# Layer-1 mixer of a two-layer decoder: the preparation split into a part of k and a part of q and v, and the chain begun once k is there

## The chip, the cores and the metric

The kernel runs on one core of a Trainium2 chip. The metric is device microseconds of one execution, median of several. TensorE (PE in the profile) does the matmuls and transposes, VectorE (DVE) and ScalarE (ACT) work on what comes out, GpSimd (POOL) does a few small powers, and the DMA issues stand on SyncE (SP).

## The reference

The program computes a decoder trunk of two layers on 256 tokens of width 1024. The change concerns the mixer of layer 1, a chunked gated DeltaNet with 8 heads of 128, in chunks of 64 tokens. Cut to what matters:

```python
def mixer_c(x, w_in, conv_w, a_log, dt_bias, norm_g, w_out):
    h = x @ w_in
    q, k, v, z, bl, al = _split(h, P1_SPLITS)
    qkv = jax.nn.silu(causal_dwconv(jnp.concatenate([q, k, v], axis=-1), conv_w))
    q, k, v = _split(qkv, P1_SPLITS[:3])
    o = gated_deltanet(q, k, v, bl, al, z, a_log, dt_bias, norm_g)
    return o @ w_out

# in gated_deltanet, per head and chunk
gc = jnp.cumsum(scal(g), axis=-1)
decay = exp(where(incl, gc[..., :, None] - gc[..., None, :], -inf))
m = jnp.where(strict, einsum('bhntk,bhnsk->bhnts', kb, kh) * decay, 0.0)
tinv = triangular_solve(eye + m, eye)
u = tinv @ (vh * beta);  w = tinv @ (kb * exp(gc))
qk = einsum('bhntk,bhnsk->bhnts', qh, kh) * decay
# then a scan over the chunks: v_new = u - w state; out = qg state + qk v_new; state update
```

The triangular inverse needs k, beta and g alone. q and v come in with `u`, `qk` and the scan.

## The kernel before, in words

Every product is made in a split form: a weight tile is cast to a short part `wh` on ACT (L151), the rest `wl` is a subtraction on DVE (L153), and three matmuls are added (L158 to L160, L164 to L166). A tile of a projection of q, k or v is 128 output columns: 24 matmuls of 256 columns on PE, one cast on ACT, one subtraction on DVE, then a scale on ACT (L926), three taps of a short convolution on DVE (L929) and a silu on ACT (L934). There are four buffers each for `wh` and `wl`, so the cast for a tile waits until PE is done with the tile four before it.

The eight heads go in two groups of four. For each group `gdn_pre` prepares (twice, for two halves of 128 tokens): `pg` is the running sum of the decay, spread out by matmuls; `pk`, `pq`, `pv` are k, q, v turned by PE transposes; `dT` is the decay (DVE L1014, then an Exp on ACT, L1016); sums of squares of k and q (`sq`, ACT L999); `LT` is the matrix k k^T times beta and decay (DVE L1052), turned into `pL`. `gdn_inv` then doubles the block of the triangular inverse in six levels, each with two half-steps on PE: `pA` and `pX`, then `pZ`; between them ACT and DVE make the operands. `gdn_rec` runs the scan over the chunks (`pvn`, `pS`, `pon`) and the norm.

`scalars` makes beta and the decays. It is a chain across the engines: a small projection, `pl` on PE (L899), Abs, Exp and Ln on ACT (L905 to L907), `gg` on DVE (L913), `pgc` on PE (L917), then two results of `pgc` on ACT (`ngc`, `egs`, L919 and L920). The four silu of the first k projection (`ck`) are held back until `egs` is out.

What sets the order: before the first `yield 0` of `mixer_c` a scheduler places the instructions of all engines. From there on `weave` fixes the order on PE as it is written: at each `yield n` of the chain, n pieces of the fill (6 matmuls of a q, k or v projection, or 3 of a z projection, each) are put on PE. `steps` runs two or three generators of the chain in turn and adds their numbers; where a generator yields nothing, the weight from the list `NW` counts. The other engines' queues are still placed by the scheduler. Each engine works through its queue in order.

Before the change, k, q and v of group 0 are projected ahead of the chain, k, q and v of group 1 are fill for the preparation and inverse of group 0, and the z projection of group 1 is fill for the preparation and inverse of group 1, in which the scan of group 0 also runs.

Of the kernel before, what the change touches and what calls it, by code (L numbers as in the profile page):

```python
# [17 lines left out]
P = 128  # L18
# [11 lines left out]
NTAIL = 8  # L30
NEARLY = 6
AHEAD = 2
NW = [3, 2.6, 1, 2.5, 1, 1.2, 0.7, 3, 2, 3, 4, 1, 6, 2, 0, 5.2, 0.3, 3]
NEG = -1e30

def _constants():
# [52 lines left out]
def hybrid_trunk(ctx: ExitStack, tc: tile.TileContext, a: dict, const: dict, out: bass.AP, dbg=None):  # L89
# [778 lines left out]
    def mixer_c(h, hT, sm, smq, fill, res):  # L868
# [127 lines left out]
        def sum_sq(dst, src):  # L996
            junk = t2("sq")
            for g in range(4):
                nc.scalar.activation(junk[:, g], src[:, g], AF.Square, accum_out=dst[:, g:g + 1])  # L999

        def gdn_pre(grp, tt, o):
            tsl = slice(tt * P, tt * P + P)
            cs = slice(tt * 8 + grp * 4, tt * 8 + grp * 4 + 4)
            q, k, v = (qkvT[x, grp][:, :, tsl] for x in "qkv")
            sc = sm.tile([P, 6, 4], F32, tag="sc", name="sc", bufs=4)

            pg = bank("pg")
            mm4(pg, lambda g: gg[:, tt, grp * 4 + g:grp * 4 + g + 1].broadcast_to([P, P]), lambda g: tri)
            pk = bank("pk")
            tr4(pk, k)  # L1010
            dT = o["att"] = keep("dT", grp, tt)
            for g in range(4):
                i = tt * 8 + grp * 4 + g
                nc.vector.scalar_tensor_tensor(dT[:, g], pg[:, g], ngc[:, i:i + 1], dmask, op0=ALU.add, op1=ALU.min)  # L1014
            with tc.issue_after(table[1].ins):
                nc.scalar.activation(dT, dT, AF.Exp)  # L1016
                if tt:
                    qg = o["qg"] = keep("kq", grp, tt)
                    nc.scalar.activation(qg, pg, AF.Exp)
            sum_sq(sc[:, 0], pk)  # L1020
            if tt:
                kgx = o["kgx"] = g2("kgx")
                tts(kgx, pk, col(egs[:, 0, cs]), op=ALU.mult)
            else:
                kg = o["kg"] = keep("kq", grp, tt)
                tts(kg, pk, col(egs[:, 1, cs]), op=ALU.mult)
            yield NW[7 + grp]
            pq = bank("pq")
            tr4(pq, q)
            sum_sq(sc[:, 1], pq)  # L1030
            pv = bank("pv")
            tr4(pv, v)

            nc.vector.tensor_scalar(sc[:, 0:2], sc[:, 0:2], RMS_EPS, None, op0=ALU.add)
            nc.gpsimd.tensor_tensor(sc[:, 2], sc[:, 0], phalf, op=ALU.pow)
            nc.vector.reciprocal(sc[:, 3], sc[:, 0])
            nc.vector.tensor_tensor(sc[:, 3], sc[:, 3], beta[:, tt, grp * 4:grp * 4 + 4], op=ALU.mult)
            nc.vector.tensor_scalar(sc[:, 4], sc[:, 1], RMS_EPS * P, None, op0=ALU.mult)  # L1040
            o["b"], o["eq"] = sc[:, 3], sc[:, 4]
            vx = o["vx"] = keep("vx", grp, tt)
            for g in range(4):
                nc.scalar.mul(vx[:, g], pv[:, g], sc[:, 2, g:g + 1])
            if tt:
                tts(qg, qg, q, op=ALU.mult)
            yield
            pK = bank("pK")
            mm4(pK, lambda g: k[:, g], lambda g: k[:, g])
            LT = t2("LT")  # L1050
            for g in range(4):
                nc.vector.scalar_tensor_tensor(LT[:, g], pK[:, g], sc[:, 3, g:g + 1], dT[:, g],  # L1052
                                               op0=ALU.mult, op1=ALU.mult)
            pQ = bank("pQ")
            mm4(pQ, lambda g: k[:, g], lambda g: q[:, g])
            tts(dT, pQ, dT, op=ALU.mult)
            yield

            pL = bank("pL")
            tr4(pL, LT)  # L1060
            L = o["L"] = t2("L")
            nc.scalar.copy(L, pL)

            Z = o["Z"] = t2("Z")
            nc.scalar.copy(Z, row(C("ident1")))
            A = level_tile()
            zu = Z.rearrange("p g (u r b) -> p g u r b", u=2, r=2)[:, :, :, 1]
            tts(A, LT.rearrange("p g (n u) -> p g n u", u=2)[..., 1], heads(C("imask")), op=ALU.mult)
            tts(zu, zu, A.rearrange("p g (b u) -> p g u b", u=2), op=ALU.subtract)
            yield  # L1070

        def gdn_inv(o):
            Z, L = o["Z"], o["L"]
            for lev in range(1, NLEV + 1):

                last = lev == NLEV
                half = slice(0, 64)
                rows = slice(64, P) if last else slice(0, P)
                cols = half if last else slice(0, P)
                Lc = smq.tile([P, 4, 64], F32, tag="Lc", name="Lc", bufs=3)  # L1080
                nc.scalar.copy(Lc.rearrange("p g (r b) -> p g r b", r=1 << lev)[rows],
                               lower(L, lev)[rows].rearrange("p g b r -> p g r b"))
                pA = mm("pA")[half, :256].rearrange("p (g t) -> p g t", g=4)
                mm4(pA, lambda g: Lc[rows, g], lambda g: Z[rows, g, 64:])
                A = level_tile()[half]
                if last:
                    nc.vector.tensor_copy(A, pA)
                else:
                    tts(A, pA, heads(cmasks[half, lev - 1]), op=ALU.mult)
                pX = bank("pX")[half, :, cols]  # L1090
                for g in range(4):
                    nc.tensor.transpose(pX[:, g], Z[cols, g, half], ident[cols, cols])
                X = t2("X")[half, :, cols]
                nc.scalar.copy(X, pX)
                if not last:
                    def packed(x):
                        return x.rearrange("p g (i u) -> p g u i", u=2)

                    Z2 = g2("Z") if lev == NLEV - 1 else t2("Z")
                    Zv = Z2.rearrange("p g (u v i) -> p g u v i", u=2, v=2)  # L1100
                    nc.scalar.copy(Zv[:, :, :, 0], packed(Z[:, :, half]))
                yield
                pZ = mm("pZ")[cols, :256].rearrange("p (g t) -> p g t", g=4)
                mm4(pZ, lambda g: X[:, g], lambda g: A[:, g])
                if last:
                    tts(Z[half, :, 64:], Z[half, :, 64:], pZ, op=ALU.subtract)
                else:
                    tts(Zv[:, :, :, 1], packed(Z[:, :, 64:]), packed(pZ), op=ALU.subtract)
                    Z = o["Z"] = Z2
                yield NW[9] if "kgx" in o and lev == NLEV else None  # L1110
            if "kgx" in o:
                pw = bank("pw")
                mm4(pw, lambda g: o["kgx"][:, g], lambda g: Z[:, g])
                wT = o["wT"] = g2("wT")
                nc.scalar.mul(wT, pw, -1.0)
# [66 lines left out]
        run(extra)  # L1182
        for finish in late:
            finish()
        proj_t(*proj_c(0, "q"))
        proj_t(*proj_c(0, "v"))

        def group_1():
            for nm in "kqv":
                yield from proj_t_gen(*proj_c(1, nm))  # L1190

        yield 0
        fill.gens.append(group_1())
        yield from steps(NW[3], gdn_pre(0, 0, os_[0][0]), gdn_pre(0, 1, os_[0][1]))
        yield from steps(NW[4], gdn_inv(os_[0][0]), gdn_inv(os_[0][1]))
        fill.rest()
        fill.gens.append(proj_z(1))
        yield from steps(NW[5], gdn_pre(1, 0, os_[1][0]), gdn_pre(1, 1, os_[1][1]))
        outs = []
        yield from steps(NW[16], gdn_inv(os_[1][0]), gdn_inv(os_[1][1]), gdn_rec(0, os_[0], outs))  # L1200
        fill.rest()
        new = new_t("oT")
        oT.hi, oT.lo = new.hi, new.lo
# [246 lines left out]
```

## Time and profile before

| | |
|---|---|
| runs | 943.89 us median of 3 (941.56 to 945.12) |
| profiled execution | 942.03 us, of which the span of instructions is 940.3 us |
| PE busy | 917.3 us (98%), 6284 matmuls |
| weight loads on PE | 820.6 us (87%) |
| DVE busy | 689.1 us (73%) |
| ACT busy | 532.6 us (57%) |
| DMA | 152.89 MB, mean 163 GB/s |

PE is the engine to follow: its queue is in order and it is hardly ever idle. A matmul's end is modelled, so one row's time is longer than the distance to the next start; the pace is read from the distance of starts. The layer-1 mixer lies between about 480 us and 688 us of the span: k, q and v of group 0 from 490.6 us to 525.7 us, the preparation of group 0 up to 551.1 us, its inverse up to 596.1 us, the preparation of group 1 up to 615.5 us, its inverse together with the scan of group 0 up to about 654 us, then the scan of group 1 between the matmuls of the output projection.

### The profile page before, as it was taken

The page shows a single profiled execution, that of the slowest core. Times are in us where ns is not written, and L with a number is a line of the kernel's source. Part 1 is how long each engine was busy: PE and PEld are TensorE (multiplying, and loading weights), DVE is VectorE, ACT ScalarE, POOL GpSimd, SP SyncE. Part 2 cuts the span into 40 slices and gives each one's busy share as a digit, 9 for nine tenths or more (in the row PEclk, how much of TensorE's full clock was granted, in tenths as well). Part 3 has the DMA queues.
Part 4 walks back from the last instruction along what each step waited for, and adds up shares of the span by engine and source line. Part 5 has one row for each costly group of instructions (what it writes and reads, how often), then busy time and mean ns, then how long its engine had stood idle before and what let it go on. Part 6 is the DMA issues. An engine that isn't in the chain of part 4 may idle for free. (4 is left out here: it accounts for less than half of the span.)

```text
span 940.3 us, 15842 instructions
## 1 busy us (share of the span) xinstructions
PE 917.3 (98%) x6284; PEld 820.6 (87%) x6284; DVE 689.1 (73%) x1155; ACT 532.6 (57%) x945; POOL 36.0 (4%) x49
## 2 busy tenths in 40 slices
PE   6999999999999999999999999999999999999996
PEld 5887798889988999998889999888889789999885
DVE  5497586776458999984687975754697889999554
ACT  4753466445444766663357876664364476666440
POOL 1000001000000000000010100000200000000000
PEclk9999999999999999999999999997999999999998
DMA  7843345555573566655566441211444546665541
GB/s 247 293 147 108 117 135 183 177 180 179 190 251 97 180 198 209 209 193 182 179 189 190 136 127 54 91 46 45 151 163 136 177 137 213 207 206 182 189 170 45
DMA packets 101715, 152.89 MB, mean 163 GB/s; under 512 B 5225, under 2 KB 73673, under 8 KB 101641
## 3 DMA queue, kind: packets, MB, share of 16 engines
q1 hardware_dynamic: 99576, 145.08, 46.9%
q0 software_dynamic: 2064, 6.80, 2.2%
q8 instruction: 50, 0.82, 0.4%
q14 instruction: 25, 0.20, 0.1%
HBM read 150.81 MB, written 1.05 MB: 162 GB/s over the span
## 5 line engine op out<-in xcount | busy, mean ns | idle before, releaser
L153 DVE TENSOR_TENSOR wl<-raw,wh 128x1024 fp32r<-128x1024 f32 x268 | 325.4, 1222 | 116.0 <-ACT wh L151 113.3
L151 ACT CAST wh<-raw 128x1024 fp32r<-128x1024 f32 x268 | 278.9, 1052 | 229.3 <-PE ps_f L159 53.1
L158 PE MATMUL ps_f<-hT,wh 128*128 128x256 f32 x576 | 159.0, 276 | 0.0
L159 PE MATMUL ps_f<-hT,wh 128*128 128x256 f32 x576 | 159.0, 276 | 0.0
L160 PE MATMUL ps_f<-hT,wl 128*128 128x256 f32 x576 | 159.0, 276 | 0.0
L158 PEld LDWEIGHTS ps_f<-hT,wh 128*128 128x128 f32 x576 | 108.1, 188 | 0.0
L159 PEld LDWEIGHTS ps_f<-hT,wh 128*128 128x128 f32 x576 | 108.1, 188 | 0.0
L160 PEld LDWEIGHTS ps_f<-hT,wl 128*128 128x128 f32 x576 | 108.1, 188 | 0.0
L158 PE MATMUL ps_t<-hT,wh 128*128 128x256 f32 x352 | 100.5, 286 | 0.0
L159 PE MATMUL ps_t<-hT,wh 128*128 128x256 f32 x352 | 97.9, 278 | 0.0
L160 PE MATMUL ps_t<-hT,wl 128*128 128x256 f32 x352 | 97.8, 278 | 0.0
L164 PE MATMUL ps_o<-wh,aT 128*128 128x512 f32 x176 | 69.2, 393 | 0.0
L165 PE MATMUL ps_o<-wl,aT 128*128 128x512 f32 x176 | 68.8, 391 | 0.0
L166 PE MATMUL ps_o<-wh,aT 128*128 128x512 f32 x176 | 68.6, 390 | 0.0
L158 PEld LDWEIGHTS ps_t<-hT,wh 128*128 128x128 f32 x352 | 66.1, 188 | 0.7
L159 PEld LDWEIGHTS ps_t<-hT,wh 128*128 128x128 f32 x352 | 66.4, 189 | 0.1
L160 PEld LDWEIGHTS ps_t<-hT,wl 128*128 128x128 f32 x352 | 66.3, 188 | 0.0
L302 PE MATMUL ps<-wh,hT 128*128 128x512 f32 x192 | 54.3, 401 | 0.0
L302 PEld LDWEIGHTS ps<-wh,hT 128*128 128x128 f32 x192 | 36.0, 191 | 8.4 <-DVE hT L381 0.5
L1311 ACT ACTIVATE fy<-ps_f,fcw 128x256 f32<-128x256 f32 x72 | 40.2, 559 | 0.0
L164 PEld LDWEIGHTS ps_o<-wh,aT 128*128 128x128 f32 x176 | 33.0, 188 | 7.6 <-issue 0.5
L166 PEld LDWEIGHTS ps_o<-wh,aT 128*128 128x128 f32 x176 | 33.0, 188 | 7.3
(359 smaller groups left out, 1843.0 us busy)
## 6 DMA issues: line engine op xcount, KB each, us to landing
raw<-in_ffn_w_in SPq DMA_DIRECT2D x44, 1024.0 KB, 5.5
raw<-in_w_in SPq DMA_DIRECT2D x26, 1024.0 KB, 5.7
raw<-in_ffn_w_out SPq DMA_DIRECT2D x22, 1024.0 KB, 5.0
raw<-in_xa_wkv SPq DMA_DIRECT2D x16, 1024.0 KB, 5.3
raw<-in_w_mix_out SPq DMA_DIRECT2D x8, 1024.0 KB, 5.1
raw<-in_xa_wq SPq DMA_DIRECT2D x8, 1024.0 KB, 7.9
raw<-in_xa_wo SPq DMA_DIRECT2D x8, 1024.0 KB, 5.0
lngb<-in_ln_g POOLq DMA_DIRECT2D x6, 512.0 KB, 4.5
```

The lines of the kernel that those rows point to most:

```text
L151: nc.scalar.copy(hi, src)
L153: nc.vector.tensor_tensor(lo, src, hi.bitcast(F32), op=ALU.subtract)
L158: nc.tensor.matmul(ps, lh, rh, start=first, stop=False)
L159: nc.tensor.matmul(ps, lh, rl, start=False, stop=False)
L160: nc.tensor.matmul(ps, ll, rh, start=False, stop=last)
L164: nc.tensor.matmul(ps, lh, rh, start=first, stop=False)
L165: nc.tensor.matmul(ps, lh, rl, start=False, stop=False)
L166: nc.tensor.matmul(ps, ll, rh, start=False, stop=last)
L302: nc.tensor.matmul(ps, x, ww[:, k], start=k0 + k == 0 and ww is wh and not xl, stop=k0 + k == KT - 1 and ww is wl)
L1311: nc.scalar.activation(yt, ps, AF.Identity, scale=cw[:, 2, mc:mc + 1], bias=cw[:, 3, mc:mc + 1])
```

## The change

`gdn_pre` becomes `gdn_pre_k`, with all that the inverse needs, and `gdn_pre_q`, with the rest (`pq`, `pv`, `pQ`). The chain starts after the k projection of group 0. One list of fill holds q and v of group 0, then k, q and v of group 1, then z of group 1; `until` gives fill until a named projection is complete. The order of the chain is k part of group 0, inverse of group 0, q part of group 0, k part of group 1, inverse of group 1 with the scan of group 0, q part of group 1. The weights in `NW` are new.

```diff
-NW = [3, 2.6, 1, 2.5, 1, 1.2, 0.7, 3, 2, 3, 4, 1, 6, 2, 0, 5.2, 0.3, 3]
+NW = [3, 2.6, 1, 1.5, 1, 1, 0.7, 1, 1, 8, 4, 1, 6, 2, 0, 5.2, 0.5, 3]
...
-        def gdn_pre(grp, tt, o):
+        def gdn_pre_k(grp, tt, o):
...
-            yield NW[7 + grp]
-            pq = bank("pq")
-            tr4(pq, q)
-            sum_sq(sc[:, 1], pq)
-            pv = bank("pv")
-            tr4(pv, v)
+            yield
-            nc.vector.tensor_scalar(sc[:, 0:2], sc[:, 0:2], RMS_EPS, None, op0=ALU.add)
+            nc.vector.tensor_scalar(sc[:, 0], sc[:, 0], RMS_EPS, None, op0=ALU.add)
...
-            pQ = bank("pQ")
-            mm4(pQ, lambda g: k[:, g], lambda g: q[:, g])
-            tts(dT, pQ, dT, op=ALU.mult)
             yield
...
+        def gdn_pre_q(grp, tt, o):
...
+            pq = bank("pq")
+            tr4(pq, q)
+            sum_sq(sc[:, 1], pq)
+            pv = bank("pv")
+            tr4(pv, v)
+            nc.vector.tensor_scalar(sc[:, 4], sc[:, 1], RMS_EPS, RMS_EPS * P, op0=ALU.add, op1=ALU.mult)
+            vx = o["vx"] = keep("vx", grp, tt)
+            for g in range(4):
+                nc.scalar.mul(vx[:, g], pv[:, g], sc[:, 2, g:g + 1])
+            if tt:
+                tts(o["qg"], o["qg"], q, op=ALU.mult)
+            yield
+            pQ = bank("pQ")
+            mm4(pQ, lambda g: k[:, g], lambda g: q[:, g])
+            tts(dT, pQ, dT, op=ALU.mult)
+            yield
...
-                yield NW[9] if "kgx" in o and lev == NLEV else None
+                yield
...
-        proj_t(*proj_c(0, "q"))
-        proj_t(*proj_c(0, "v"))
+        made = set()
+        def fills():
+            for grp in range(2):
+                for nm in "kqv"[1 - grp:]:
+                    yield from proj_t_gen(*proj_c(grp, nm))
+                    made.add((nm, grp))
+        def until(nm, grp):
+            while (nm, grp) not in made:
+                yield 1
...
         yield 0
-        fill.gens.append(group_1())
-        yield from steps(NW[3], gdn_pre(0, 0, os_[0][0]), gdn_pre(0, 1, os_[0][1]))
-        yield from steps(NW[4], gdn_inv(os_[0][0]), gdn_inv(os_[0][1]))
-        fill.rest()
-        fill.gens.append(proj_z(1))
-        yield from steps(NW[5], gdn_pre(1, 0, os_[1][0]), gdn_pre(1, 1, os_[1][1]))
+        fill.gens += [fills(), proj_z(1)]
+        yield from units(NW[3], gdn_pre_k, 0)
+        yield from inv(NW[4], 0)
+        yield from until("v", 0)
+        yield from units(NW[7], gdn_pre_q, 0)
+        yield from until("k", 1)
+        yield from units(NW[5], gdn_pre_k, 1)
         outs = []
-        yield from steps(NW[16], gdn_inv(os_[1][0]), gdn_inv(os_[1][1]), gdn_rec(0, os_[0], outs))
+        yield from steps(NW[8], *(gdn_inv(os_[1][tt]) for tt in range(2)), gdn_rec(0, os_[0], outs))
+        yield from until("v", 1)
+        yield from units(NW[8], gdn_pre_q, 1)
         fill.rest()
```

**PE, the start of the chain.** Before, the scalars' `pl` is followed by the q projection of group 0 (`ps_t`), and 49 of its matmuls stand between `pl` and `pgc`; another 143 stand between `pgc` and `pg`.

```order
L899 MATMUL pl<-c_all,linT 128x16 x4
L158 MATMUL ps_t<-hT,wh 128x256
L159 MATMUL ps_t<-hT,wh 128x256
L160 MATMUL ps_t<-hT,wl 128x256
...
L917 MATMUL pgc<-gg,c_m_4955 128x16 x2
L159 MATMUL ps_t<-hT,wh 128x256
L160 MATMUL ps_t<-hT,wl 128x256
```

In the change, on PE from `pl` on:

```order
L899 MATMUL pl<-c_all,linT 128x16 x4
L917 MATMUL pgc<-gg,c_m_4955 128x16 x2
L986 MATMUL pg<-c_m_4955,gg 128x128 x4
L982 MATMUL pk<-c_all,ck 128x128 x4
L986 MATMUL pg<-c_m_4955,gg 128x128 x4
L982 MATMUL pk<-c_all,ck 128x128 x4
L158 MATMUL ps_t<-hT,wh 128x256
```

The q and v projections of group 0 (192 matmuls) have moved behind `pk`; nothing stands between `pl`, `pgc`, `pg` and `pk`. Then 18 `ps_t` matmuls come before `pK`, and 18 more between `pK` and `pL`.

**ACT, the same place.** In the change, from the Exp of the scalars (L906) to the first Exp of the decay:

```order
L906 ACTIVATE gtmp<-gtmp 128x16
L907 ACT_TABLE_LOAD
L907 ACTIVATE gtmp<-gtmp 128x16
L919 ACTIVATE ngc<-pgc 128x16
L920 ACT_TABLE_LOAD
L920 ACTIVATE egs<-pgc 128x32
L934 ACT_TABLE_LOAD
L934 ACTIVATE ck<-cv 128x256 x4
L999 ACTIVATE sq,sc<-pk 128x128
L1017 ACT_TABLE_LOAD
L1017 ACTIVATE dT<-dT 128x512
```

Before, a cast (L151) stood between L906 and the first table load, and a scale and a cast between L907 and `ngc`; these have moved back, the three table loads have not.

**DVE, the first `LT`.** In the change, on DVE, where `LT` of the two token halves is made (the first four of L1040 are of the first half, the last four of the second):

```order
L1040 SCALAR_TENSOR_TENSOR LT<-pK,sc,dT 128x128 x2
L1024 TENSOR_TENSOR kgx<-pk,egs 128x512
L1040 SCALAR_TENSOR_TENSOR LT<-pK,sc,dT 128x128 x2
L1031 TENSOR_SCALAR sc<-sc 128x4
L1053 TENSOR_TENSOR A<-LT,c_m_4955 128x256
L1033 RECIPROCAL sc<-sc 128x4
L153 TENSOR_TENSOR wl<-raw,wh 128x1024
L1034 TENSOR_TENSOR sc<-sc,beta 128x4
L929 SCALAR_TENSOR_TENSOR cv<-ps_t,gcw,cv 128x253
L1040 SCALAR_TENSOR_TENSOR LT<-pK,sc,dT 128x128 x4
```

A weight split (`wl`) and a convolution tap (`cv`) of the fill have come in between the first and the second half's `LT`.

**PE, the last levels of group 1.** Before, the z projection is used up and the last half-steps follow each other:

```order
L986 MATMUL pZ<-A,X 128x64 x8
L986 MATMUL pA<-Z,Lc 64x64 x4
L1092 MATMUL pX<-c_all,Z 64x64 x4
L986 MATMUL pA<-Z,Lc 64x64 x4
L1092 MATMUL pX<-c_all,Z 64x64 x4
L986 MATMUL pZ<-A,X 64x64 x8
L986 MATMUL pw<-Z,kgx 128x128 x4
```

In the change 12 matmuls of the q and v projections of group 1 stand at each half-step (18 at three of them), of which the first and last rows are shown:

```order
L986 MATMUL pA<-Z,Lc 64x64 x4
L1101 MATMUL pX<-c_all,Z 64x128 x4
L158 MATMUL ps_t<-hT,wh 128x256
L159 MATMUL ps_t<-hT,wh 128x256
L160 MATMUL ps_t<-hT,wl 128x256
...
L986 MATMUL pZ<-A,X 128x64 x8
```

The z projection has moved behind these, between `pw` and the scan of group 1. Beside this ACT has two table loads more: one for the silu of the q and v projections of group 1 (L934), one for the softmax of the cross-attention that follows (L1275 of the change, L1252 before).

## Rows read from the trace of the kernel before

**Rows 1.** Busy time by stage: stretch, PE, PEld, DVE, ACT, POOL, clock, DMA, GB/s
```profile
490.60:502.00 11.40, 11.40 (x99) 11.27 (x97) 8.89 (x14) 5.60 (x9) 0.00 (x0) 1.00 0.82 232
525.70:551.10 25.40, 24.09 (x208) 23.53 (x207) 22.77 (x57) 21.89 (x67) 2.88 (x2) 1.00 0.41 122
551.10:596.10 45.00, 45.00 (x411) 41.22 (x411) 26.62 (x54) 27.89 (x55) 0.00 (x0) 1.00 0.29 95
596.10:615.50 19.40, 17.43 (x116) 14.94 (x114) 14.55 (x40) 16.28 (x57) 2.02 (x2) 1.00 0.17 56
615.50:643.20 27.70, 27.11 (x231) 23.36 (x231) 12.21 (x26) 17.34 (x47) 2.01 (x2) 1.00 0.11 39
648.20:658.50 10.30, 9.74 (x59) 9.09 (x60) 3.43 (x7) 2.70 (x5) 0.00 (x0) 0.50 0.19 70
```

**Rows 2.** What PE waited for from 500 to 690 us: total, times, longest
```profile
PE pK L986 <- ACT vx L1044: 1.2, 1, 1.2
PE pq L982 <- ACT kq L1019: 1.0, 1, 1.0
PE pA L986 <- ACT Lc L1081: 0.7, 1, 0.7
```

**Rows 3.** PE in order of time: start, time, line, count
```profile
501.99 1.06 PE L899 MATMUL pl<-c_all,linT 32*128 32x16 f32 x8
...
509.01 0.59 PE L917 MATMUL pgc<-gg,c_m 128*128 128x16 f32 x4 [0.19 <-issue]
...
525.75 1.05 PE L986 MATMUL pg<-c_m,gg 128*128 128x128 f32 x8
526.64 0.60 PE L982 MATMUL pk<-c_all,ck 128*128 128x128 f32 x4
527.08 1.06 PE L986 MATMUL pg<-c_m,gg 128*128 128x128 f32 x8
```

**Rows 4.** ACT in order of time around the scalars
```profile
505.04 0.22 ACT L906 ACTIVATE gtmp<-gtmp 128x16 f32<-128x16 f32 x1
505.91 1.05 ACT L151 CAST wh<-raw 128x1024 fp32r<-128x1024 f32 x1 [0.66 <-PE ps_t L159]
506.98 1.28 ACT L907 ACT_TABLE_LOAD   x1
508.28 0.22 ACT L907 ACTIVATE gtmp<-gtmp 128x16 f32<-128x16 f32 x1
...
512.67 1.34 ACT L934 ACTIVATE ck<-cv 128x256 f32<-128x256 f32 x4
```

**Rows 5.** DVE in order of time, first preparation: a split, LT, a tap
```profile
538.51 1.22 DVE L153 TENSOR_TENSOR wl<-raw,wh 128x1024 fp32r<-128x1024 f32 x1 [0.29 <-ACT wh L151]
539.66 1.12 DVE L1052 SCALAR_TENSOR_TENSOR LT<-pK,sc,dT 128x128 f32<-128x128 f32 x4
...
542.67 0.48 DVE L929 SCALAR_TENSOR_TENSOR cv<-ps_t,gcw,cv 128x253 f32<-128x253 f32 x1 [1.10 <-ACT cv L926]
```

**Rows 6.** DVE in order of time, start of group 1's scan
```profile
656.39 1.61 DVE L1144 SCALAR_TENSOR_TENSOR oT<-pz,ng,oT 128x512 fp32r<-128x512 f32 x2 [3.74 <-ACT oT L1143]
658.23 0.69 DVE L1124 TENSOR_TENSOR vn<-pvn,sc 128x512 f32<-128x512 f32 x1 [0.23 <-PE pvn L986]
```

**Rows 7.** ACT in order of time at the first softmax of cross-attention
```profile
708.47 1.05 ACT L151 CAST wh<-raw 128x1024 fp32r<-128x1024 f32 x1 [2.77 <-PE ps_t L159]
709.42 0.47 ACT L1252 ACTIVATE xp<-xs,xst 128x256 f32<-128x256 f32 x1
```

**Rows 8.** DVE at the same place
```profile
711.09 0.68 DVE L1255 TENSOR_TENSOR xp<-xp,xst 128x512 f32<-128x512 f32 x1
```

**Rows 9.** PE at the same place
```profile
711.91 0.63 PE L1261 MATMUL xt<-c_all,xp 128*128 128x128 f32 x4
```

More of the change, by code (lines that the diff above doesn't have):

```diff
@@ L990, in level_tile @@
         def level_tile():
-            return smq.tile([P, 4, 64], F32, tag="A", name="A")
+            return smq.tile([P, 4, 64], F32, tag="A", name="A", bufs=2)
         def heads(x):
@@ L999, in sum_sq @@
                 nc.scalar.activation(junk[:, g], src[:, g], AF.Square, accum_out=dst[:, g:g + 1])
-        def gdn_pre(grp, tt, o):
+        def gdn_pre_k(grp, tt, o):
             tsl = slice(tt * P, tt * P + P)
             cs = slice(tt * 8 + grp * 4, tt * 8 + grp * 4 + 4)
-            q, k, v = (qkvT[x, grp][:, :, tsl] for x in "qkv")
-            sc = sm.tile([P, 6, 4], F32, tag="sc", name="sc", bufs=4)
+            k = qkvT["k", grp][:, :, tsl]
+            sc = o["sc"] = sm.tile([P, 6, 4], F32, tag="sc", name="sc", bufs=4)
             pg = bank("pg")
@@ L1039, in gdn_pre @@
             nc.vector.tensor_tensor(sc[:, 3], sc[:, 3], beta[:, tt, grp * 4:grp * 4 + 4], op=ALU.mult)
-            nc.vector.tensor_scalar(sc[:, 4], sc[:, 1], RMS_EPS * P, None, op0=ALU.mult)
             o["b"], o["eq"] = sc[:, 3], sc[:, 4]
[L1042 to L1047, printed above, removed]
             pK = bank("pK")
@@ L1069, in gdn_pre @@
             tts(zu, zu, A.rearrange("p g (b u) -> p g u b", u=2), op=ALU.subtract)
+            yield
+        def gdn_pre_q(grp, tt, o):
+            tsl = slice(tt * P, tt * P + P)
+            q, k, v = (qkvT[x, grp][:, :, tsl] for x in "qkv")
+            sc, dT = o["sc"], o["att"]
+            pq = bank("pq")
[13 more added lines that the diff above has]
+            tts(dT, pQ, dT, op=ALU.mult)
             yield
@@ L1184, in mixer_c, with units, inv @@
             finish()
-        proj_t(*proj_c(0, "q"))
-        proj_t(*proj_c(0, "v"))
-        def group_1():
-            for nm in "kqv":
-                yield from proj_t_gen(*proj_c(1, nm))
-        yield 0
-        fill.gens.append(group_1())
-        yield from steps(NW[3], gdn_pre(0, 0, os_[0][0]), gdn_pre(0, 1, os_[0][1]))
-        yield from steps(NW[4], gdn_inv(os_[0][0]), gdn_inv(os_[0][1]))
-        fill.rest()
-        fill.gens.append(proj_z(1))
-        yield from steps(NW[5], gdn_pre(1, 0, os_[1][0]), gdn_pre(1, 1, os_[1][1]))
+        made = set()
[7 more added lines that the diff above has]
+                yield 1
+        def units(n, gen, grp, *args):
+            return steps(n, *(gen(grp, tt, os_[grp][tt]) for tt in range(2)))
+        def inv(n, grp):
+            return steps(n, *(gdn_inv(os_[grp][tt]) for tt in range(2)))
+        yield 0
+        fill.gens += [fills(), proj_z(1)]
[5 more added lines that the diff above has]
+        yield from units(NW[5], gdn_pre_k, 1)
         outs = []
-        yield from steps(NW[16], gdn_inv(os_[1][0]), gdn_inv(os_[1][1]), gdn_rec(0, os_[0], outs))
+        yield from steps(NW[8], *(gdn_inv(os_[1][tt]) for tt in range(2)), gdn_rec(0, os_[0], outs))
+        yield from until("v", 1)
+        yield from units(NW[8], gdn_pre_q, 1)
         fill.rest()
```

## The prediction

> **What bounds the kernel now.** I read the page's busy times first, then the busy time by stage, then what PE waited for, then the order of time at the start of the chain. PE bounds: the page has it busy 98% of the span, and its queue is in order. So the time is the sum of PE's own work and of what it loses, and a change that neither adds nor removes matmuls can only move the losses. This one keeps the matmuls: the same projections, transposes and products stand in another order. So I count what PE loses in the stretch now, and then what it will lose.
>
> The losses now [rows 1]: the first preparation, 525.7 to 551.1 us, is 25.40 us with PE busy 24.09, so 1.31 idle. The inverse of group 0, with 12 matmuls of fill at each half-step, is 45.00 us with PE busy all of it: that density of fill hides the chain. The preparation of group 1 loses 19.40 - 17.43 = 1.97, its levels 27.70 - 27.11 = 0.59, and the end, 648.2 to 658.5 us, 10.30 - 9.74 = 0.56. Together 4.43 us idle. The last row shows something else: the granted clock is 0.50 there, that is 1.2 GHz instead of 2.4. What went before is the end of the levels, where the z projection is used up and PE has only the small matmuls of the chain. At full clock the 9.74 us of work would take half if all of it scaled, so the clock costs at most 4.87 us. **All that there is to win is 4.43 + 4.87 = 9.3 us.** I take the whole of it as won (bounds: from 5, the idle time alone with a little of the clock, to 9.3).
>
> **The change part by part.** *The start of the chain.* Before, PE has 192 matmuls of the q and v projections around `pgc` and ahead of `pg`; now nothing stands between `pl` and `pk`. What `pk` waits for is a chain over ACT, DVE and PE that the change does not shorten: Ln after a table load, `gg` on DVE, `pgc`, `ngc`, a table load, `egs`, a table load, the four silu of `ck` that wait behind `egs`. In the trace it runs from the first table load at 506.98 us to the end of the silu, 512.67 + 1.34 = 514.01: 7.03 us [rows 4]. The start moves up: the Exp before it ends at 505.04 + 0.22 = 505.26, and the cast that stood between (until 506.96, after a wait for PE) is gone. So `ck` is there at 505.26 + 7.03 = 512.3 us. PE is through with `pl` at about 503.05 (501.99 + 1.06) [rows 3] and has until then only `pgc`, whose next matmul starts 0.44 later, and one `pg`, 526.64 - 525.75 = 0.89. PE stands idle for 512.3 - 503.05 - 1.33 = **7.9 us**. Below it could be 7.0, since a scale and a cast are also gone from ACT between Ln and `ngc` and the first transpose of `pk` needs only the first silu; above 9.3, if `pg` came late too.
>
> *The clock after that.* A spell without work of this length in the trace's middle is not to be seen; the waits of 1.2 and 1.0 us [rows 2] left the clock at 1.00 in their stretches, and thin work before 648.2 us took it to 0.50 for 10.3 us [rows 1]. Idle time is thinner than any of this, so I take it that the clock falls. A spell of 10.3 us that begins somewhere in the idle stretch of 9.3 us lies on average half in it, where it costs nothing, and half in work, at half speed: 10.3 / 2 / 2 = 2.6 us lost. It may end sooner, since dense work follows: I take **2.1 us**; bounds 0 (no fall) and 5.1 (all of the spell in work).
> The Trainium skill, "TensorE: Matmul & The Clock Gate" (section "HAM oscillation"), says that a long enough gap without matmuls puts the engine back to half rate, and that it has to be busy again for a while before it is released; this speaks against a change that opens a gap. By that rule the fall is sure; no row here shows an idle gap with a fall behind it.
>
> *The first LT.* With `pk` at time 0, PE does `pk`, `pg`, `pk` in 0.44 + 0.89 + 0.44 = 1.8 us, 18 `ps_t` at 11.40 / 96 = 0.119 us [rows 1] in 2.1, `pK` (two like `pg`) in 1.8, then 18 more in 2.1: it is at `pL` at 7.8, and at its second half at 8.2. The second half's `LT` stands on DVE behind the split of a fill tile. That split needs a cast, which needs the buffer of the first q tile, whose 24 matmuls end at 1.8 + 2.1 + 1.8 + 0.7 = 6.4. Cast 1.05 [rows 4], split 1.22, tap 0.48, `LT` 1.12 [rows 5]: 6.4 + 3.9 = 10.3. PE waits 10.3 - 8.2 = **2.1 us**; bounds 0 (if the split is already through) and 3. Behind this wait stand the fill and all of the inverse.
>
> *Three shorter covers.* `pv` of group 0 and `pk` of group 1 now come 6 `ps_t` (0.7 us) and one small product behind the last matmul of the projection that they read, and scale, three taps and silu of that tile lie between: three taps of 0.48 [rows 5] and a quarter of 1.34 [rows 4] alone are 1.8 us. `pL` of group 1 has 12 matmuls before it where the first time 18 were too few. The nearest rows are the waits in the preparation before, 1.2 and 1.0 us [rows 2]: 3 x 1.1 = **3.3 us**; bounds 0 and 6, twice as long each.
>
> *The scan of group 1.* `pS` now follows `pvn` with no matmul of the output projection between. It needs `vn`, 0.69 on DVE, which stands behind two `oT` of 1.61 together [rows 6], while PE has the second `pvn`, 0.89 (as `pg`) [rows 3]: **0.7 us**; bounds 0 and 1.6.
>
> *Two table loads more on ACT.* A switch takes 1.30 us, from 506.98 to the start of the Ln at 508.28 [rows 4]. The one for silu lies in the levels of group 1, whose `pZ` comes 18 matmuls and a `pvn` later: nothing, as ACT was busy only 17.34 of 27.70 us there [rows 1]. If that cover is gone it costs 1.3. The one for the softmax does not hide: it stands behind the cast that ends at 709.5 us [rows 7], and the chain from there to `xp`, done at 711.77 [rows 8], ends only 0.14 us before `xt` starts at 711.91 [rows 9]. So 1.30 - 0.14 = **1.2 us**; bounds 0 and 1.3.
> By the Trainium skill, "ScalarE: Activation LUTs" (section "What ACT_TABLE_LOAD costs"), a switch has a drain behind the load and takes about 2.66 us in all; the row shows the next activation at 1.30, so the sum goes by the row. By the page's figure the two would be an estimated 2.7 us dearer together.
>
> *What I cost at nothing.* The levels of group 1 with more fill: in the inverse of group 0 the same 12 matmuls, casts and taps run beside the same levels with PE never idle [rows 1]. Moving the z projection back: its gate is read first in the norm of group 1's scan. The DMA issues on SP keep their order (k, q, v, z, output projection), and DMA is busy less than half of these stretches [rows 1].
>
> **The sum.** 7.9 + 2.1 + 2.1 + 3.3 + 0.7 + 1.2 = 17.3 us lost, 9.3 won: 8.0 us slower. Against the profiled execution, 942.03 us (span 940.3 and 1.7 around it), that is 950.0; the median of the runs is 1.9 above that execution, so I predict **952.0 us**.
>
> **The rivals.**
> 1. *The clock stays at half for as long as it did before.* The spell of 10.3 us falls wholly behind `pk`: 5.1 instead of 2.1, so 955.0 us. For it: the length in [rows 1]. Against: there thin work went on under it, here dense fill follows. By the Trainium skill (the page and section named above) the release comes after a while of steady work, which speaks for less.
> 2. *The second group's stretch pays for all* (the other side). Place: 596.1 to 658.5 us. The dense fill gives back the 9.3 us, the clock does not fall at the start, and the casts and splits that are gone from the queues let the first `LT` and the three shorter covers come in time; only the 7.9 us stays. 943.9 + 7.9 - 9.3 = 942.5 us, not slower. It decides once the other losses are below 1.4 us. For it: the inverse of group 0 loses nothing [rows 1]. Against: the covers are shorter than those that lost 1.2 and 1.0 before [rows 2].
> 3. *The levels of group 1 are not hidden* (the change then doesn't do what it says). They now carry splits and taps and the scan of group 0 too: DVE was busy 26.62 of 45.00 us in the inverse of group 0, and here the scan's six or so operations of 0.69 come on top. If each of the 12 half-steps waits 0.5 us, as the 0.7 us wait of `pA` [rows 2], it is 6 us more: 958.0. Against: 27 + 4 of 45 us is still no bound.
>
> **How the numbers follow.** Chances: the forecast 0.50, rival 1 0.20, rival 2 0.15, rival 3 0.15. Range: the lowest sum of the bounds is 7.0 - 9.3, 941.6, the highest beyond 960; leaving about one in ten on either side gives 946 to 958, the upper end at rival 3. About 0.5%, 4.7 us, is what a measurement of this kernel can tell from no change. Slower by more than that, over 948.6: nearly all of the forecast, rivals 1 and 3, 0.83. Within: most of rival 2 and the lowest of the forecast, 0.13. Faster by more needs the 7.9 us to be less than 4.6 with no other loss: 0.04.
>
> **What would show it.** A wait of PE before `pgc` and one before `pk`, together about 8 us, right after `pl`; the silu of `ck` ending near 512 us; a clock of 0.50 soon after, and of 1.00 in the end of group 1; a wait before the second half of the first `pL`; a table load before the first softmax with `xt` waiting for `xp`. I am wrong if PE goes from `pl` to `pk` with less than 5 us idle, or if the stretch from `pk` on has more to win than the 9.3 us counted here.

## The result and the profile after

The change made the kernel slower: 954.02 us (median of 4 runs, 953.16 to 957.59) beside 942.95 us (4 runs, 941.56 to 945.12), a ratio of 1.0123, 95% interval [1.0089, 1.0156]. The profiled execution took 954.16 us, of which the span is 952.4 us: 12.1 us more than before. PE is busy for 920.2 us (97%) where it was 917.3, with the same 6284 matmuls: 9.2 of the 12.1 us are time in which PE stood still, and 2.9 are the same work done more slowly.

What PE waited for in the whole stretch of the change, the answer to [rows 2] (total, times, longest):

```profile
PE pgc L917 <- issue: 4.2, 1, 4.2
PE pk L982 <- ACT ck L934: 4.1, 2, 2.4
PE pv L982 <- ACT cv L934: 2.1, 2, 1.9
PE pL L982 <- DVE LT L1040: 1.3, 1, 1.3
PE xt L1284 <- DVE xp L1278: 0.9, 1, 0.9
PE pS L986 <- DVE vn L1133: 0.7, 1, 0.7
PE ps L302 <- DVE hT L381: 0.5, 1, 0.5
PE pA L986 <- ACT Lc L1090: 0.4, 1, 0.4
```

Of the waits in [rows 2] only that of `pA` is left, and new ones stand at every joint that the change made. The first is put down to "issue", but DVE in order of time shows the operand: `gg` is written at 506.59 + 0.18 us, and `pgc` starts at 506.87.

```profile
506.59 0.18 DVE L913 SCALAR_TENSOR_TENSOR gg<-gtmp,ab 128x16 f32<-128x16 f32 x1
```

The start of the chain on PE in order of time (in brackets the idle time ahead), the answer to [rows 3]:

```profile
501.56 1.06 PE L899 MATMUL pl<-c_all,linT 32*128 32x16 f32 x8
506.87 1.01 PE L917 MATMUL pgc<-gg,c_m 128*128 128x16 f32 x4 [4.25 <-issue]
507.72 2.05 PE L986 MATMUL pg<-c_m,gg 128*128 128x128 f32 x8
511.38 1.40 PE L982 MATMUL pk<-c_all,ck 128*128 128x128 f32 x4 [1.60 <-ACT ck L934]
512.57 1.91 PE L986 MATMUL pg<-c_m,gg 128*128 128x128 f32 x8
514.27 1.06 PE L982 MATMUL pk<-c_all,ck 128*128 128x128 f32 x4
514.98 0.56 PE L158 MATMUL ps_t<-hT,wh 128*128 128x256 f32 x1
```

`pg`'s eight matmuls take 0.89 us from start to start in [rows 3]; here the second `pg` takes 514.27 - 512.57 = 1.70. The busy time by stage says why (stretch, PE, PEld, DVE, ACT, POOL, clock, DMA, GB/s; the answer to [rows 1]):

```profile
506.10:516.30 10.20, 7.82 (x34) 7.18 (x35) 2.99 (x11) 8.00 (x22) 0.00 (x0) 0.50 0.26 87
...
591.50:594.80 3.30, 3.30 (x18) 3.30 (x17) 1.01 (x3) 3.27 (x16) 0.00 (x0) 0.50 0.35 135
604.00:650.00 46.00, 46.00 (x418) 42.54 (x416) 26.61 (x55) 28.35 (x69) 2.01 (x2) 1.00 0.21 70
```

The granted clock fell to 0.50 (1.2 GHz) twice in the mixer: from 506.1 us, 3.5 us into the idle stretch behind `pl`, and from about 591.4 us, behind the 2.4 us wait of group 1's `pk`. The last row is the other side of the account: from 604 us on the levels of group 1 run without a gap at full clock.

On ACT the start is the forecast chain, three table loads (two of them shown) and the silu, answering [rows 4]:

```profile
504.84 1.28 ACT L907 ACT_TABLE_LOAD   x1
...
509.61 1.28 ACT L934 ACT_TABLE_LOAD   x1
510.91 1.34 ACT L934 ACTIVATE ck<-cv 128x256 f32<-128x256 f32 x4
```

### The profile page after: what moved, and what is told of

Read it like the earlier page. It is cut to its first block, busy times and chain, and to the rows that moved or that the text cites. A ratio compares the mean times of both kernels' runs of the same rounds, so it can differ in the third digit from the quotient of the medians.

```text
span 952.4 us, 15826 instructions
## 1 busy us (share of the span) xinstructions
PE 920.2 (97%) x6284; PEld 823.0 (86%) x6284; DVE 690.4 (72%) x1155; ACT 536.8 (56%) x947; POOL 35.2 (4%) x49
## 3 DMA queue, kind: packets, MB, share of 16 engines
HBM read 150.81 MB, written 1.05 MB: 159 GB/s over the span
## 5 line engine op out<-in xcount | busy, mean ns | idle before, releaser
L151 ACT CAST wh<-raw 128x1024 fp32r<-128x1024 f32 x268 | 279.2, 1052 | 237.7 <-PE ps_f L159 52.8
L158 PE MATMUL ps_t<-hT,wh 128*128 128x256 f32 x352 | 102.5, 291 | 0.0
L159 PE MATMUL ps_t<-hT,wh 128*128 128x256 f32 x352 | 98.5, 280 | 0.0
L302 PE MATMUL ps<-wh,hT 128*128 128x512 f32 x192 | 55.3, 406 | 0.5 <-DVE hT L381 0.5
L302 PEld LDWEIGHTS ps<-wh,hT 128*128 128x128 f32 x192 | 36.3, 193 | 9.0 <-DVE hT L381 1.2
```

Source lines behind the costliest of these rows:

```text
L151: nc.scalar.copy(hi, src)
L158: nc.tensor.matmul(ps, lh, rh, start=first, stop=False)
L159: nc.tensor.matmul(ps, lh, rl, start=False, stop=False)
L302: nc.tensor.matmul(ps, x, ww[:, k], start=k0 + k == 0 and ww is wh and not xl, stop=k0 + k == KT - 1 and ww is wl)
```

## The experiments

All but `e8_lt_first` and `e10_Z_first` were made to explain the result; ratios are to the kernel before, run beside them. It took 941.2 to 941.6 us there and 942.95 beside the change, so a difference to the change's 954.02 us is uncertain by more than 1 us.

**`e1_q_ahead`: the q projection of group 0 back ahead of the chain, the rest of the change kept.**

```diff
+        proj_t(*proj_c(0, "q"))
         made = set()
...
-                for nm in "kqv"[1 - grp:]:
+                for nm in ("v", "kqv")[grp]:
```

> The changed kernel with one thing undone: the q projection of group 0 (96 matmuls) stands ahead of the chain again, v and all of group 1 stay fill. Theory (PE loses at the start because nothing stands between pl and pk, and at pv of group 0 and pk of group 1 because the projection they read has only just ended): the 8.3 us idle between pl and pk goes, with it the half clock after it (about 2 us), and since the fill is 96 matmuls ahead, v of group 0 and k of group 1 are long done when pv and pk read them (2.1 and 2.8 us, and the second fall of the clock, 1.3 us): 954 - 15 = 937 to 941 us, below the kernel before. Rival (the loss at the start only moves: what q covers is lost again where the fill runs out): the last levels of group 1 show a clock of 0.50 again and the time is 943 to 947 us.

Measured: 940.85 us, ratio 0.9997 [0.9988, 1.0007]. All that the change lost comes back with this one edit: 13.2 us by the medians, some 12 when each kernel is set against the kernel before that ran beside it, and so more than the start alone is worth. PE's longest wait is now

```profile
PE pL L982 <- DVE LT L1040: 2.1, 1, 2.1
```

The waits of `pgc` and `pk` at the start are gone, and so are those of `pv` and of group 1's `pk`. With 96 matmuls less in the fill of group 0, v of group 0 and k of group 1 are projected well before they are turned, so nothing is read just as it ends.

**`e2_idle_filled`: the idle stretch filled with matmuls of no use**, 33 ahead of `pgc` and 26 ahead of the first `pk`.

```diff
+        def idle_work(n):
+            ps = mm("idle")[:, :T]
+            for _ in range(n):
+                nc.tensor.matmul(ps, hT.h(0)[:, :P], hT.h(1), start=True, stop=True, skip_group_check=True)
...
+            if not grp and not tt:
+                idle_work(26)
             pk = bank("pk")
```

> The changed kernel with 33 matmuls of no use (256 columns, result not read) between pl and pgc and 26 between pg and the first pk, in PE's idle time; it does more work than the changed kernel, not less. Theory (the idle time costs 8.3 us by itself and the half clock that follows it 2 us more): the chain over ACT and DVE still ends with the silu of ck near 512 us, the granted clock stays at 1.00 there, and the time falls by the clock's share alone: 952.0 us. Rival A (the clock's fall costs nothing, since PE waits for LT anyway): 954.0 us. Rival B (the clock's fall is the greater part): 949 us or less.

Measured: 953.75 us, ratio 1.0146 [1.0110, 1.0182], the time of the change itself. By stage:

```profile
504.50:516.00 11.50, 11.38 (x95) 11.02 (x95) 4.78 (x15) 9.12 (x21) 0.00 (x0) 1.00 0.37 107
516.00:528.00 12.00, 9.59 (x86) 9.04 (x84) 9.85 (x30) 10.44 (x30) 2.03 (x2) 1.00 0.01 1
```

The clock stays at 1.00 here, and PE now stands still 12.00 - 9.59 = 2.4 us in the next stretch, nearly all of it where `pA` waits for `Lc`. PE in order of time:

```profile
503.47 1.06 PE L899 MATMUL pl<-c_all,linT 32*128 32x16 f32 x8
...
528.27 0.68 PE L986 MATMUL pA<-Z,Lc 128*64 128x64 f32 x8 [2.13 <-ACT Lc L1092]
...
530.82 0.43 PE L986 MATMUL pZ<-A,X 64*128 64x64 f32 x2
```

The first `pZ` of the change:

```profile
530.21 0.99 PE L986 MATMUL pZ<-A,X 64*128 64x64 f32 x7
```

From `pl` to the first `pZ` it is 27.35 us with the idle time filled; in the change it is 530.21 - 501.56 = 28.65. So 1.3 us hang on the slower clock up to there, and 1.7 us up to the end of the span (952.6 - 503.47 = 449.1 against 952.4 - 501.56 = 450.8), near the 2 us of the theory. The equal medians don't speak against this. In this execution `pl` came 1.9 us later than in the change, most of it behind a stretch at 0.50 near 110 us, in work that the edit doesn't touch; the change's execution had no such stretch there:

```profile
110.30:113.70 3.40, 3.40 (x18) 3.40 (x17) 0.74 (x2) 0.59 (x1) 0.00 (x0) 0.50 0.92 307
```

The four runs of each spread over more than that, so the runs don't decide between 952.0 and 954.0 us. Either way the clock is the small part: behind the start a chain over three engines bounds, and PE at full speed gets through it hardly sooner.

**`e3_fill_in_gap`: useful fill in the same places**, 30 matmuls between `pl` and `pgc`, 30 between `pg` and `pk`.

```diff
         fill.gens += [fills(), proj_z(1)]
+        yield 5
+        run(extra)
+        for finish in late + early:
+            finish()
...
+            if not grp:
+                yield 2.5
             pk = bank("pk")
```

> The changed kernel with its own fill in the two idle stretches: five pieces of fill (30 matmuls of the q projection) between pl and pgc, five between pg and pk. The chain still begins once k is there. Theory (what is missing is fill between pl and pk): 60 matmuls, 7.0 us, of the idle time are used, less what the casts and taps of these tiles put into the scalars' chain on ACT and DVE (before it ended at 514.0 instead of 512.3 us, so up to 2 us), and the clock's fall goes: 945 to 948 us. Rival (the fill's casts and taps hold up the scalars by as much as it covers): 951 us or more.

Measured: 947.14 us, ratio 1.0063 [1.0048, 1.0078]. 6.9 us are back by the medians, with `pgc` still waiting 2.3 us and group 1's `pk` 2.4, by PE's waits:

```profile
PE pk L987 <- ACT ck L934: 2.4, 1, 2.4
PE pgc L917 <- issue: 2.3, 1, 2.3
```

The theory was wrong on the clock: it fell here too, at the wait of `pgc`, as the busy time by stage shows.

```profile
507.20:514.00 6.80, 6.62 (x31) 6.65 (x32) 3.67 (x12) 4.62 (x10) 0.00 (x0) 0.50 0.06 18
```

Not all of the 6.9 us come from the start. PE in order of time, `pl` and the first fill behind the second `pk`:

```profile
500.37 1.06 PE L899 MATMUL pl<-c_all,linT 32*128 32x16 f32 x8
...
517.05 0.36 PE L158 MATMUL ps_t<-hT,wh 128*128 128x256 f32 x1
```

That is 16.68 us, of which the 60 matmuls of fill are 7.1 at 0.119; 9.5 are left, where the change has 514.98 - 501.56 = 13.42. So 3.9 us are won at the start. The rest lies behind it: `pv` waits 0.2 us where it waited 2.1, the first `pL` no longer waits its 1.3, and the second fall of the clock is gone; against that `pA` waits 1.4 us in all where it waited 0.4.

Beside `e2_idle_filled` this is the control: the same places filled with work that had to be done anyway pay, even under a slower clock; filled with other work they pay little or nothing. So it is mainly the idle time, and not what it does to the clock, that made the change slower there.

**`e4_later_covers`: 24 matmuls more of fill ahead of `pv` of group 0, 30 more ahead of `pk` of group 1.**

```diff
         yield from until("v", 0)
+        yield 4
...
         yield from until("k", 1)
+        yield 5
```

> The changed kernel with four more pieces of fill (24 matmuls) ahead of pq and pv of group 0 and five more (30) ahead of pg and pk of group 1; the start is left as it is. Theory (these waits come from reading a projection that has only just ended): pv 2.1, pk 2.8 and the second fall of the clock 1.3 us go: 954 - 6 = 948 us. Rival (the fill is only moved and is missing at the end): the last levels of group 1 lose as much, clock 0.50 near 650 us, 953 to 956 us.

Measured: 953.56 us, ratio 1.0129 [1.0114, 1.0144]: nothing won. Both waits that it aimed at went, and a larger one came up in the next step. PE's waits:

```profile
PE pL L982 <- DVE LT L1040: 4.7, 2, 3.4
```

The place on PE in order of time:

```profile
587.40 0.60 PE L982 MATMUL pk<-c_all,ck 128*128 128x128 f32 x4
...
597.80 1.25 PE L982 MATMUL pL<-c_all,LT 128*128 128x128 f32 x4 [3.42 <-DVE LT L1040]
```

The second half's `LT` on DVE ends 11.1 us behind the first `pk`'s start, and PE had 24 `ps_t`, `pK` and little more to do in between:

```profile
597.40 1.13 DVE L1040 SCALAR_TENSOR_TENSOR LT<-pK,sc,dT 128x128 f32<-128x128 f32 x4
```

The clock is then at 0.50 for 10.2 us, by the busy time of that stretch:

```profile
597.10:607.30 10.20, 8.40 (x44) 7.08 (x45) 5.76 (x15) 7.83 (x14) 0.00 (x0) 0.50 0.33 103
```

So my theory's price for these two covers fell: a wait taken away in front of a chain that is itself not covered only moves behind it. The time is the rival's, but the loss did not go to the end of the levels, as the rival had it.

**`e7_deeper_cover_grp1`: the same, and 30 in place of 12 matmuls at each step of group 1's k part.**

```diff
-NW = [3, 2.6, 1, 1.5, 1, 1, 0.7, 1, 1, 8, 4, 1, 6, 2, 0, 5.2, 0.5, 3]
+NW = [3, 2.6, 1, 1.5, 1, 2.5, 0.7, 1, 1, 8, 4, 1, 6, 2, 0, 5.2, 0.5, 3]
```

> The run with covers ahead of pv and of group 1's pk, and besides 30 in place of 12 matmuls of fill at each step of the k part of group 1. Theory (the exposed chain from pk to the second LT, 11 us against 32 matmuls, is what took back the two waits won): the 4.7 us wait of pL and the clock's fall behind it go, 945 to 949. Rival (the wait is moved once more, to the steps behind, which have less fill): 951 to 955.

Measured: 948.40 us, ratio 1.0074 [1.0058, 1.0091]. The same chain from `pk` to `LT` is now covered, 5.2 us are won, and the stretch after it stays at full clock (busy time by stage):

```profile
600.00:610.00 10.00, 8.77 (x80) 8.11 (x80) 9.27 (x16) 8.20 (x18) 0.00 (x0) 1.00 0.52 183
```

The 1.23 us idle in this row are the fill's: a `ps_t` matmul waits for its own split `wl` on DVE. The start is as in the change (`pgc` waits 4.2 us, `pk` 1.6), and the kernel is still 7.2 us above the 941.22 us of the kernel before beside it.

**`e5_thicker_k_part`: on `e1_q_ahead`, 30 and 24 in place of 18 and 12 matmuls at the steps of the two k parts** (NW[3] 2.5, NW[5] 2.2).

> q's projection ahead of the chain as in the run that put it there, and besides 30 in place of 18 matmuls of fill at each step of the k part of group 0, and 24 in place of 12 at each step of the k part of group 1. Theory (the k part is a chain of ScalarE and VectorE some 8 to 11 us long, and what it costs is what TensorE's fill does not cover of it): of the run with q ahead, at 940.9, the 4.7 us lost at the first k part's steps (wait for LT, a slower clock at its matmuls) and the 1.1 to 1.6 at the second one's go, 934 to 937. Rival (the fill is one sum: what is used early is missing late): the fill is used up before the last steps of group 1's q and v part, their waits come back at the price of what was won, 939 to 942.

Measured: 943.57 us, ratio 1.0027 [1.0013, 1.0041]: slower than `e1_q_ahead`, and beyond what either theory had. The rival's wait at the end is there (`pw`, 1.0 us), but the larger part isn't the fill that is missing late: `pL` waits longer, not shorter, though PE has more to do before it. PE's waits:

```profile
PE pL L982 <- DVE LT L1040: 4.1, 2, 2.5
PE pw L986 <- DVE Z L1115: 1.4, 2, 1.0
```

DVE of `e1_q_ahead` in order of time, behind the products with egs and up to `LT`:

```profile
520.60 1.22 DVE L153 TENSOR_TENSOR wl<-raw,wh 128x1024 fp32r<-128x1024 f32 x1
...
521.87 1.22 DVE L153 TENSOR_TENSOR wl<-raw,wh 128x1024 fp32r<-128x1024 f32 x1
...
524.34 2.15 DVE L1040 SCALAR_TENSOR_TENSOR LT<-pK,sc,dT 128x128 f32<-128x128 f32 x8
```

The same place of this run:

```profile
520.57 1.22 DVE L153 TENSOR_TENSOR wl<-raw,wh 128x1024 fp32r<-128x1024 f32 x1
...
522.81 1.22 DVE L153 TENSOR_TENSOR wl<-raw,wh 128x1024 fp32r<-128x1024 f32 x1
...
525.02 1.20 DVE L153 TENSOR_TENSOR wl<-raw,wh 128x1024 fp32r<-128x1024 f32 x1
...
526.28 1.22 DVE L153 TENSOR_TENSOR wl<-raw,wh 128x1024 fp32r<-128x1024 f32 x1
527.42 2.15 DVE L1040 SCALAR_TENSOR_TENSOR LT<-pK,sc,dT 128x128 f32<-128x128 f32 x8
```

The fill brings its own splits, and they stand ahead of `LT` in DVE's queue: two more of them, and `LT` starts 3.1 us later. More fill covers a chain only as long as the fill's own work isn't in the chain's way.

**`e6_table_and_pS`: on `e5_thicker_k_part`, a dummy Exp behind group 1's preparation and 6 matmuls between `pvn` and `pS`.**

```diff
-NW = [3, 2.6, 1, 2.5, 1, 2.2, 0.7, 1, 1, 8, 4, 1, 6, 2, 0, 5.2, 0.5, 3]
+NW = [3, 2.6, 1, 2.5, 1, 2.2, 1, 1, 1, 8, 4, 1, 6, 2, 0, 5.2, 0.5, 3]
...
+        warm = sm.tile([P, 4], F32, name="warm", bufs=1)
+        nc.scalar.activation(warm, os_[1][1]["eq"], AF.Exp, scale=0.0)
```

> The run before this one, with two edits: a dummy Exp of one column on ScalarE behind group 1's q-and-v preparation, so that the softmax's table is there before its first Exp, and a thin step of the output projection between pvn and pS. Theory: the wait of xt for xp (0.9) and of pS for vn (0.7) go, 1.0 to 1.6 us less than the run without these edits. Rival (the Exp's wait is for the cast and the matmul ahead of it and not for the table; vn's chain goes on to the next step): within 0.5 of it.

Measured: 943.45 us, ratio 1.0020 [1.0009, 1.0030], the rival's time. The waits of `xt` and `pS` are both gone from PE's list. The table load now stands at the dummy Exp and no longer ahead of the softmax, so it was what `xt` waited for; but a wait of 0.6 us of `pt` for `h` is new, and the clock was at half for 3.4 us behind 650.5 us in this profile. With two edits in one run, what took back the 1.6 us can't be told apart.

**`e8_row` and `e8_lt_first`: `LT` ahead of the fill's splits.** The first, a control on `e1_q_ahead`, makes the projections of q and v one row of fill, so that v's first splits are asked for during q; the second then puts splits that are asked for between `pk` and `LT` behind `LT` on DVE (`low` is the subtraction of a split). The code shown is that of the second.

```diff
+            lows[0] = tt == 1
             yield
...
+            if tt:
+                lows[0] = False
+                for low in lows[1:]:
+                    low(last)
+                del lows[1:]
```

> The control of the next run: q ahead as before, and q's and v's projections of group 0 made as one row, so that v's first two splits are asked for while q is computed. VectorE has two splits between the products with egs and LT as in the run with q ahead. Theory (LT of group 0 is late by what stands before it on VectorE): nothing changes, pL waits about 2 us for LT, within 0.5 of the run with q ahead (940.9 beside a before of 941.6), 940 to 941.5. Rival (v's start is late for its loads): 1 to 2 less.

> The control with one more edit: the splits of the fill that are asked for between pk and LT are put on VectorE behind LT. Theory: LT's four operations for the first half end some 2.4 us earlier (two splits of 1.22), pL's wait of 2.1 us goes and with it the slower clock behind it (1 to 1.5), 2 to 3.5 us less than the control, 937 to 939. Rival (the fill then waits for its own split, or LT waits for dT's Exp behind its table load): pL's wait goes down by under 1 us or comes back at ps_t, within 0.7 of the control.

Measured: the control 940.96 us, ratio 0.9996 [0.9983, 1.0009]; with `LT` first 938.94 us, ratio 0.9971 [0.9961, 0.9982]. The medians differ by 2.0 us, the two profiled spans only by 0.7 (938.6 and 937.9). So what is won lies between 0.7 and 2 us. `LT` starts at 521.81 instead of 524.56 us, and `pL` no longer waits. PE of the control in order of time:

```profile
525.05 2.19 PE L1000 MATMUL pL<-c_all,LT 128*128 128x128 f32 x8 [2.08 <-DVE LT L1058]
```

PE with `LT` first:

```profile
522.97 1.39 PE L1009 MATMUL pL<-c_all,LT 128*128 128x128 f32 x8
528.23 0.65 PE L1013 MATMUL pA<-Z,Lc 128*64 128x64 f32 x8 [1.75 <-DVE Z L1087]
```

The wait moved by one step, to the first level's `Z`, which now stands behind the held splits on DVE. The slower clock did not go, as the theory had it, but moved along (0.50 from 525.5 us in the control, from 529.3 us here). This is the one version that beats both kernels, the one before by 0.3%.

**`e10_Z_first`: the held splits behind the first level's `A` and `Z` as well** (the block above, moved one step on).

> The run with LT first, and the held splits put behind the first level's A and Z as well. Theory (the wait moved on to the next operation of the chain that stands behind the fill's splits on VectorE): pA's wait of 1.8 us for Z goes, and the slower clock behind it, 1.5 to 2.5 us less than that run, 936.5 to 937.5. Rival (the fill's own matmuls then wait for the held splits, or the wait moves on again to Lc on ScalarE): within 0.7 of it, 938.2 to 939.6.

Measured: 940.01 us, ratio 0.9985 [0.9969, 1.0001], 1.1 us slower than the run before and 0.4 above the rival's range. Now the fill waits for its own split, as the rival had it (PE in order of time).

```profile
527.64 0.39 PE L169 MATMUL ps_t<-hT,wl 128*128 128x256 f32 x1 [2.31 <-DVE wl L157]
```

In these three versions another order on DVE only hands a wait of about 2 us (2.08, 1.75, 2.31) from one step to the next. That DVE's work in this stretch bounds is likely, but not shown.

## Why the prediction was right, and where a size was off

The direction and the mechanism held: slower, 954.0 us against 952.0 forecast, within the range. The time came nearer than the account: 11.1 us slower by the medians and 12.1 by the spans, against 8.0 forecast, and the kernel before ran 0.9 us faster here than the 943.89 us that I had started from. That part is luck. By the distance of starts against the pace of the same matmuls in [rows 1, 3]:

- *Start of the chain.* Forecast 7.9 us. From `pl` to the second `pg` it is 512.57 - 501.56 = 11.01 us, and at PE's pace 0.99 + 0.44 + 0.89 + 0.44 = 2.76: 8.25 us. `ck` was complete at 510.91 + 1.34 = 512.25, forecast 512.3; here two errors cancel, since the chain from the first table load began 0.4 us sooner (504.84 against 505.26) and took 0.4 longer (7.41 against 7.03). `e3_fill_in_gap` shows that it was real time: 3.9 us of it came back with fill in its place, and `e1_q_ahead` leaves no wait there above 0.2 us.
- *The clock.* The fall came, and its work behind `pk` is 0.81 (`pg`), 0.27 (`pk`) and 0.64 (18 `ps_t`, from 514.98 to 517.76) longer: 1.7 us against 2.1. As a price of its own it is worth 1.3 us up to the first `pZ` and 1.7 up to the end of the span (`e2_idle_filled`), since part of what follows waits for DVE and ACT. By the rule of the Trainium skill ("TensorE: Matmul & The Clock Gate", section "HAM oscillation") the fall was sure, and the trace agrees: it came 3.5 us into the idle stretch.
- *The first LT.* From `pL`'s start at 521.60 to the next fill at 524.27 it is 2.67 us, 1.8 over the pace; idle 1.3. Forecast 2.1, at the place and by the split that the prediction named.
- *Three shorter covers.* **This is the term that was mis-sized: 3.3 us, with a bound of 6. The waits cost 4.9, and 6.4 with the slower clock that one of them brought.** `pv` lost 2.1 and group 1's `pk` 2.8 (idle 1.9 and 2.4, for the last quarter of a silu), `pL` of group 1 nothing; the second fall of the clock, which I had not counted, cost 1.5 us in the second `pk` and 12 `ps_t`. I took the price from the waits of 1.2 and 1.0 us in [rows 2], which are of another kind. The taps and the silu that I had listed, 1.8 us, with the scale of 0.47 would not have given it either: 6 `ps_t`, `pg` and three of `pk`'s matmuls cover 0.7 + 0.9 + 0.3 = 1.9 of these 2.3 us. What I left out stands among them in the queues: the cast of the next fill tile, 1.05 us, ahead of the scale on ACT, and its split, 1.23 us, ahead of the taps on DVE (rows below; at `pv` it is the same). `e1_q_ahead` shows where it comes from: chain and projections arrive together, and with 96 matmuls less to wait for it is gone.
- *`pS`* lost 0.9 us (wait 0.7) against 0.7, *the softmax* 0.9 against 1.2; the silu's table load cost nothing, as forecast. A wait of 0.5 us at L302 and about 1.0 in the output projection and `pv` of group 1 were not forecast.
- *The gain.* 9.3 us were taken as won. In the levels of group 1 nothing is lost any more: PE is busy 46.00 us of 46.00 at full clock. (Before 604 us the first level's `pA` waits 0.4.) But the clock's part of the gain was an upper bound: at the pace of the same matmuls elsewhere the stretch from 648.2 us had lost 3.9 us, its waits included, where I had 4.87 for the clock and 0.56 for the waits. So the losses above are about 21.5 us, and what was won is the idle 1.31 + 1.97 + 0.59 of [rows 1] and these 3.9, 7.8 and not 9.3. That makes 13.7 us, where the span shows 12.1 and I had 8.0; the 1.6 us between are not accounted for.

ACT and DVE of the change in order of time for group 1's first `pk`, from the end of the k projection to the silu that `pk` waits for:

```profile
585.76 1.05 ACT L151 CAST wh<-raw 128x1024 fp32r<-128x1024 f32 x1 [1.10 <-PE ps_t L159]
586.72 0.47 ACT L926 ACTIVATE cv<-ps_t,gcw 128x256 f32<-128x256 f32 x1
586.84 1.23 DVE L153 TENSOR_TENSOR wl<-raw,wh 128x1024 fp32r<-128x1024 f32 x1 [0.17 <-ACT wh L151]
...
589.85 0.42 ACT L934 ACTIVATE ck<-cv 128x256 f32<-128x256 f32 x1 [2.36 <-DVE cv L929]
```

Rival 1, a clock at half for all of its 10.3 us behind `pk`, fell: half of it lay in idle time. Rival 2 fell: the clock did fall, the covers did not hold, and the gain was 7.8 us and not the 9.3 that it counted. Rival 3, levels that are not hidden, fell: the only waits are 0.4 us at the first `pA` and 0.3 at `pw`.

`e5_thicker_k_part` and `e8_lt_first` say what is behind the k part's steps: `pk` to `LT` is a chain of some 9 to 13 us over ACT and DVE (first `pk` to the end of `LT`: 8.9 us in `e8_lt_first`, 11.1 in `e4_later_covers`, 12.8 in the change), and DVE's queue holds the fill's splits too. That was in the prediction for one `LT` and one split; that it holds for the taps ahead of `pv` and `pk` and for the other steps of the preparation, I had not seen. Open stays why in `e4_later_covers` ACT has two of the second half's sums of squares, which `LT` needs, behind the Exp of the decay (the scheduler places ACT's queue), and what took back the two waits in `e6_table_and_pS`.

## What to carry to other kernels

Splitting off a part of a preparation so that a chain can begin earlier pays only if the chain's first steps have work beside them: count what PE has between a projection's end and the first product that needs it, and compare it with the scale, taps, silu and table loads in between, and with the casts and splits of the fill that stand among them. The same holds at each later joint where a chain reads what a fill has just finished; give it distance. A projection's worth, 96 matmuls, was enough in `e1_q_ahead`; with the 60 of `e3_fill_in_gap` the wait of group 1's `pk` stayed at 2.4 us. And fill isn't free on the other engines: what each 24 matmuls bring to VectorE and ScalarE stands in the queues that the chain goes through, so thicker fill can delay what it is to cover.

## What the runs showed of the hardware

- A wait put down to "issue" (4.2 us before `pgc`) ended 0.1 us behind the DVE operation that wrote its operand; it was a wait for data.
- Gaps without matmuls went with the clock at 0.50 for 10.2 us (at 4.25 us idle in the change, at 3.4 us in `e4_later_covers`), 6.8 us (at 2.3 us in `e3_fill_in_gap`) or 3.4 us (at 2.4 us in the change). With the 4.25 us filled by matmuls of no use the first fall did not come, and from `pl` to the end of the span the kernel took 1.7 us less.
- Behind shorter waits it went either way. Behind `pL`'s 2.1 us in `e1_q_ahead` the clock fell (row below), behind `pA`'s 2.1 us in `e2_idle_filled` it did not (1.00 from 528.3 to 540 us). Near 110 us the same work behind the same wait of 1.24 us ran at 0.50 in the execution of `e2_idle_filled` and at 1.00 in that of the change, so one execution doesn't show what a short wait costs.

```profile
525.30:528.70 3.40, 3.40 (x16) 2.99 (x16) 3.28 (x10) 2.66 (x5) 0.00 (x0) 0.50 0.78 270
```
